# Moving small TensorE products into the beat of a recurrence step

## The chip, the cores and the metric

The kernel runs on one core of a Trainium2 chip. The metric is device time in microseconds (us) of one execution: 2334.18 us is the median of three runs of the kernel before, which lie between 2333.84 and 2334.26 us. The change does the same work; only the order in which its instructions are issued differs.

## The reference

Two layers work on 512 tokens of width 2048 in float32. The first layer projects the normalised input onto a forgetting attention (16 heads) and an RWKV-7 time mix (16 heads of size 64); the second is a gated MLP with a mixing over tokens. Each layer ends with an output projection, a second norm and a gated per-layer embedding. What the change touches is the time mix, which the reference writes as a scan over tokens with a 64x64 state `S` per head:

```python
def step(S, inp):
    r_t, w_t, k_t, v_t, kk_t, a_t = inp
    sa = jnp.einsum('bhij,bhj->bhi', S, kk_t)
    S = S * w_t[:, :, None, :] - sa[..., None] * (kk_t * a_t)[:, :, None, :] + v_t[..., None] * k_t[:, :, None, :]
    y = jnp.einsum('bhij,bhj->bhi', S, r_t)
    return S, y
```

Its outputs are normalised per head, a bonus term is added, and the result is gated and projected.

## The kernel before, in words

**Dense products.** Every projection is a stream of 128x128 weight blocks. SP loads a raw block, ACT rounds it to `whi` (L163), DVE computes the rest `wlo = raw - whi` (L165), and TensorE adds three products per block into a PSUM bank: `whi` with the high part of the activations (L179), `whi` with the low part (L180), `wlo` with the high part (L181). One such triple is called a **beat** here. One tile of `whi` or `wlo` holds four blocks, so it serves four beats, twelve dense matmuls; there are four buffers of each.

**The time mix by chunks.** The scan is turned into chunks of 64 tokens, two heads at a time, so a **period** is one of eight pairs of heads with eight chunks. For a pair there are:

- `rwkv_prep` (11 steps): decay, sigmoid gates, norms. Its products are the two LoRA products (L321) and a block sum (L302). On ACT it has a table load, sigmoids (L356, L360), a second table load (L332) and exponentials (L393, L398: `Pd`); on DVE among others the clamp of the block sum (L376), `kk` (L378), L382 and L383.
- `rwkv_ops` (4 steps for each half of the chunks): DVE alone, the scaled operands `BK` (L419, L420) and `AR` (L422, L425).
- `rwkv_head` (2 steps for each half): eight products of 64x128 tiles (L445) into two PSUM banks `tm` and `g`, and their masks on DVE (L449 to L462).
- `rwkv_inverse` (11 steps): inverts eight triangular 64x64 blocks for each head by doubling. A step is one burst of 32 products of 32x32 tiles (L512), four of them on different diagonal blocks behind each other; the result goes through DVE (`X` at L521, the transposed `T` at L529) and ACT (`R` at L530) into the next burst. The last two bursts have 16 products (L512 with `A` as an operand, and the last with `R` and `X`), and write `Tfin` through ACT (L541, L545; `X` by DVE at L538 and ACT at L539).
- `rwkv_tokens` (one step for each half): transposes to token-major form (L476, L484), copied by ACT (L478, L487, L488).
- `rwkv_chain` (three steps for each of eight chunks, 24 in a period): the recurrence. Step one is L558 and its copy `Bs` (DVE L561 and ACT L562), step two is L565 and its copy `UV` (L567, L568), step three is L573 with the new state `SV` (DVE L577), and the outputs L582 and L583.
- `rwkv_fin` (7 steps): head norm and bonus with block sums (L302).

**What sets the order.** The dense products carry a counter of beats. Each small step has a place, a number of beats, and `beat` runs every step whose place has come, right behind the dense triple of that beat:

```python
def beat(self):
    self.beats += 1
    while self.side and self.side[0][0] <= self.beats:
        self.side.pop(0)[1]()
```

The places are tables in units of `WIN` = 36 beats; a period is two of these, 72 beats. `CHAIN` puts a step of the chain every third beat. `STAGE` (inverse), `FIN`, `HEAD`, `TOKENS`, `PREP` and `OPS` hold the others; those with a 1 at the end are for the first period. All steps of all periods stand in one sorted list:

```python
def put(pr, n, step):
    todo.append((1 + 2 * WIN * pr + n, step))
```

So a period holds steps of four pairs at once: the chain of pair `pr`, the end (`FIN`) of pair `pr - 1`, heads and inverse of pair `pr + 1`, and the preparation of pair `pr + 2`. Behind this the Tile framework orders instructions by its own estimate of readiness and by priorities (copies of the chain and of the inverse are raised), so a step may be issued some matmuls away from its beat. The engines' queues then run in that order: an instruction that waits holds up those behind it.

Of the kernel before, what the change touches and what calls it, by code (L numbers as in the profile page):

```python
# [39 lines left out]

WIN = 36
even = lambda n, first, last: [WIN * (first + (last - first) * k / (n - 1)) for k in range(n)]
STAGE = even(11, 0.8, 1.94)
CHAIN = even(12, 0.06, 0.98), even(12, 1.06, 1.98)
FIN = even(7, 0.1, 0.9)
PREP = even(11, 1.3, 1.78)
PREP1 = even(11, 0.0, 0.24)
OPS = even(4, 1.83, 1.97), even(4, 0.06, 0.28)
OPS1 = even(4, 0.27, 0.38), even(4, 0.42, 0.56)
HEAD = even(2, 0.03, 0.18), even(2, 0.4, 0.6)  # L50
HEAD1 = even(2, 0.41, 0.48), even(2, 0.6, 0.7)
TOKENS = [1.03 * WIN], [0.02 * WIN]

WARM = 12

# [17 lines left out]
class Net:  # L73
# [542 lines left out]
    def rwkv_all(self, dense, first, wp, ps):  # L616
# [46 lines left out]
        def put(pr, n, step):  # L663
            todo.append((1 + 2 * WIN * pr + n, step))

        def run(pr, make, *args_places):
            *args, places = args_places
            gen = []

            def step():  # L670
                if not gen:
                    gen.append(make(*args))
                next(gen[0], None)

            for n in places:
                put(pr, n, step)
            put(pr, places[-1], lambda: [0 for _ in gen[0]])

        def begin(pr):
            S0 = sts[pr]["hf", 0]["SV"][:, 0]  # L680
            for q in range(2):
                nc.gpsimd.memset(S0[q * 64 : q * 64 + 64, q, :], 0.0)
            sts[pr]["Yt"] = self.t(wp, [P, T], "Yt")

        for pr in range(8):
            put(pr, CHAIN[0][0], lambda pr=pr: begin(pr))
            run(pr, tokens, pr, 1, TOKENS[1])
            for h in range(NG):
                run(pr, chain, pr, h, CHAIN[h])
            if pr > 0:  # L690
                run(pr, fin, pr - 1, FIN)
            if pr < 7:
# [4 lines left out]
                for h in range(NG):  # L697
                    run(pr, head, pr + 1, h, (HEAD if pr else HEAD1)[h])
                run(pr, inverse, pr + 1, STAGE)
                run(pr, tokens, pr + 1, 0, TOKENS[0])  # L700
            if pr < 6:
# [772 lines left out]
```

## Time and profile before

| what | us |
|---|---|
| median of three runs | 2334.18 |
| the profiled execution's own time | 2334.16 |
| its span, first to last instruction | 2332.5 |
| TensorE busy in the span | 2306.9 (99%) |
| VectorE (DVE) busy | 1234.6 (53%) |
| ScalarE (ACT) busy | 1043.2 (45%) |
| GpSimd (POOL) busy | 277.8 (12%) |
| first step of the chain, period 0 | starts at 142.2 |
| first step of the chain, periods 1 to 7 | 222.6, 296.7, 373.4, 447.4, 524.1, 598.2, 671.0 |
| last burst of the inverse (L512) | 666.2 |

The time outside the span is 1.7 us and is the same work in both kernels. The stretch that the tables shape runs from about 130 to 750 us. A matmul's end in the profile is modelled, so its start, and the distance to the next start, is what to read; "x64" behind L512 means 32 products, since every float32 product stands as two records.

### The profile page before, as it was taken

To read this page: it belongs to the slowest core of one execution; us is meant where nothing else is said; L and a number is where in the kernel's file an instruction comes from. 1 tells how busy PE (TensorE), PEld (TensorE's weight loads), DVE (VectorE), ACT (ScalarE), POOL (GpSimd) and SP (SyncE) were. 2 spreads that over 40 slices of the span, in tenths; PEclk is the share of its full clock that TensorE was granted. 3 is DMA by queue.
4 is the path that set the end of the run, shared out by engine and by line. 5 is a ranking of instruction groups with operands and counts; after the bars stand their busy time and mean duration, and the time that the engine had idled before them with its cause. 6 is when DMAs were issued, how large, how long until landed. Compare 5 with 4: busy or idle time off the path is not lost.

```text
span 2332.5 us, 38949 instructions
## 1 busy us (share of the span) xinstructions
PE 2306.9 (99%) x15380; PEld 1898.4 (81%) x15380; DVE 1234.6 (53%) x2526; ACT 1043.2 (45%) x2134; POOL 277.8 (12%) x314
## 2 busy tenths in 40 slices
PE   8999999999999999999999999999999999999999
PEld 7777887778887788778888888888888888888889
DVE  8665656656533877862246553237544443226433
ACT  5445554555443666753354343223333332335322
POOL 3111111111100000000112110003442000110000
PEclk9999999999999999999999999999999999999999
DMA  6322232223234533343333333334443332332332
GB/s 227 89 76 75 63 85 78 72 65 83 73 96 142 153 92 103 96 127 121 93 105 102 100 100 91 100 98 105 109 107 97 100 99 93 97 108 91 109 117 91
DMA packets 300341, 235.03 MB, mean 101 GB/s; under 512 B 11485, under 2 KB 251246, under 8 KB 299134
## 3 DMA queue, kind: packets, MB, share of 16 engines
q1 hardware_dynamic: 300158, 232.54, 34.3%
q8 instruction: 121, 1.98, 0.3%
q14 instruction: 62, 0.51, 0.1%
HBM read 216.47 MB, written 16.02 MB: 100 GB/s over the span
## 4 chain that ended last, share of the span: by engine, by line
PE 92%; DVE 4%; DMA 2%; ACT 2%; issue 1%; POOL 0%; SPq 0%; ACTq 0%; DVEq 0%; POOLq 0%
PE mm L179 16%; PE mm L181 15%; PE mm L180 15%; PE mm L940 6%; PE mm L939 6%; PE mm L941 6%; PE mm L218 5%; PE mm L217 5%; PE mm L216 5%; PE tm L512 2%; PE tm L855 1%; PE g L867 1%; DMA gz<-gd 1%; PE mm L1172 1%; DVE wlo L165 1%
## 5 line engine op out<-in xcount | busy, mean ns | idle before, releaser
L165 DVE TENSOR_TENSOR wlo<-raw,whi 128x512 fp32r<-128x512 f32 x720 | 516.5, 722 | 739.5 <-ACT whi L163 701.0
L163 ACT CAST whi<-raw 128x512 fp32r<-128x512 f32 x720 | 445.9, 621 | 889.4 <-PE mm L180 350.0
L179 PE MATMUL mm<-xh,whi 128*128 128x512 f32 x1120 | 468.3, 418 | 0.0
L181 PE MATMUL mm<-xh,wlo 128*128 128x512 f32 x1120 | 441.7, 394 | 1.2 <-DVE wlo L165 1.2
L180 PE MATMUL mm<-xl,whi 128*128 128x512 f32 x1120 | 439.2, 392 | 0.0
L181 PEld LDWEIGHTS mm<-xh,wlo 128*128 128x128 f32 x1120 | 210.2, 188 | 48.1 <-DVE wlo L165 1.6
L179 PEld LDWEIGHTS mm<-xh,whi 128*128 128x128 f32 x1120 | 211.5, 189 | 35.8
L180 PEld LDWEIGHTS mm<-xl,whi 128*128 128x128 f32 x1120 | 211.5, 189 | 31.9
L179 PE MATMUL mm<-yh,whi 128*128 128x512 f32 x576 | 225.9, 392 | 0.0
L181 PE MATMUL mm<-yh,wlo 128*128 128x512 f32 x576 | 224.4, 389 | 0.0
L180 PE MATMUL mm<-yl,whi 128*128 128x512 f32 x572 | 222.6, 389 | 0.0
L941 PE MATMUL mm<-xh,wlo 128*128 128x512 f32 x384 | 149.4, 389 | 0.0
L939 PE MATMUL mm<-xh,whi 128*128 128x512 f32 x384 | 149.4, 389 | 0.0
L940 PE MATMUL mm<-xl,whi 128*128 128x512 f32 x384 | 149.4, 389 | 0.0
L1094 POOL TENSOR_TENSOR accq<-accq,sq 128x512 f32<-128x512 f32 x42 | 56.7, 1349 | 608.7 <-ACT sq L1092 607.6
L181 PEld LDWEIGHTS mm<-yh,wlo 128*128 128x128 f32 x576 | 108.1, 188 | 22.8
L179 PEld LDWEIGHTS mm<-yh,whi 128*128 128x128 f32 x576 | 108.1, 188 | 22.1
L180 PEld LDWEIGHTS mm<-yl,whi 128*128 128x128 f32 x572 | 107.4, 188 | 22.0
L216 PE MATMUL mm<-whi,xh 128*128 128x512 f32 (+1 forms) x320 | 111.2, 347 | 0.0
L218 PE MATMUL mm<-whi,xl 128*128 128x512 f32 (+1 forms) x320 | 110.9, 347 | 0.0
L217 PE MATMUL mm<-wlo,xh 128*128 128x512 f32 (+1 forms) x320 | 110.9, 347 | 0.0
L216 PE MATMUL mm<-whi,yh 128*128 128x512 f32 x256 | 99.7, 389 | 0.0
(383 smaller groups left out, 3749.1 us busy)
## 6 DMA issues: line engine op xcount, KB each, us to landing
raw<-in_ab_w_in_dram SPq DMA_DIRECT2D x128, 512.0 KB, 4.0
raw<-in_c_w_in_dram SPq DMA_DIRECT2D x96, 512.0 KB, 3.7
raw<-in_ple_w_gate_dram SPq DMA_DIRECT2D x64, 512.0 KB, 3.9
raw<-in_ab_w_out_dram SPq DMA_DIRECT2D x32, 512.0 KB, 3.9
raw<-in_c_w_out_dram SPq DMA_DIRECT2D x32, 512.0 KB, 3.9
gd<-wlo SPq DMA_DIRECT2D x21, 256.0 KB, 2.2
xt<-in_x_dram SPq DMA_DIRECT2D x4, 1024.0 KB
xd<-xT SPq DMA_DIRECT2D x4, 1024.0 KB, 3.9
```

The lines of the kernel that those rows point to most:

```text
L163: nc.scalar.copy(hi[:, : m * n], src)
L165: self.weng.tensor_tensor(lo[:, : m * n], src, f(hi[:, : m * n]), ALU.subtract)
L179: nc.tensor.matmul(acc, hi, xhi[k], start=(k == 0), stop=False)
L180: nc.tensor.matmul(acc, hi, xlo[k], start=False, stop=False)
L181: nc.tensor.matmul(acc, lo, xhi[k], start=False, stop=(k == nk - 1))
L216: nc.tensor.matmul(accs[m][:, :n], xh, hi, start=(j == 0), stop=False)
L217: nc.tensor.matmul(accs[m][:, :n], xh, lo, start=False, stop=False)
L218: nc.tensor.matmul(accs[m][:, :n], xl, hi, start=False, stop=(j == nk - 1))
L939: nc.tensor.matmul(accs[j], hi[:, js], xhi[k], start=(k == 0), stop=False)
L940: nc.tensor.matmul(accs[j], hi[:, js], xlo[k], start=False, stop=False)
L941: nc.tensor.matmul(accs[j], lo[:, js], xhi[k], start=False, stop=(k == nk - 1))
L1094: eng.tensor_tensor(accq, accq, sq, ALU.add)
```

## The change

Four tables change, and a helper table appears. `BEHIND` is the list of the chain's 24 places, each plus 0.01 beat, so a step that is put there stands in the same beat as a step of the chain and behind it in the sorted list.

```diff
-STAGE = even(11, 0.8, 1.94)
 CHAIN = even(12, 0.06, 0.98), even(12, 1.06, 1.98)
-FIN = even(7, 0.1, 0.9)
+
+BEHIND = [n + 0.01 for half in CHAIN for n in half]
+STAGE = [0.6 * WIN, *BEHIND[8:18]]
+FIN = [4, BEHIND[2], 11, BEHIND[5], 20, 21, BEHIND[7]]
 PREP = even(11, 1.3, 1.78)
...
-HEAD = even(2, 0.03, 0.18), even(2, 0.4, 0.6)
+HEAD = [BEHIND[0], 6.5], [BEHIND[4], 20]
 HEAD1 = even(2, 0.41, 0.48), even(2, 0.6, 0.7)
-TOKENS = [1.03 * WIN], [0.02 * WIN]
+TOKENS = [BEHIND[20]], [BEHIND[1]]
```

In beats of a period: the eleven inverse steps stood at 28.8 to 69.84, every 4.1 beats, and stand at 21.6 and then 26.26 to 53.22, every third beat. The heads stood at 1.08 and 6.48, 14.4 and 21.6, and stand at 2.17 and 6.5, 14.21 and 20. The transposes of a pair's first half move from 37.08 to 62.26, those of the second half from 0.72 to 5.18. The seven end steps stood at 3.6, 8.4, 13.2, 18.0, 22.8, 27.6 and 32.4, and stand at 4, 8.19, 11, 17.22, 20, 21 and 23.25. `PREP` and `OPS` stay where they are. Instructions of each kind and their number are the same on every engine.

Counted over the order on PE from the first to the last step of the chain, the dense stream is broken by small products in 280 places before and in 223 after. Names below carry running numbers; line numbers of the change are two higher than those of the kernel before.

On PE, the end of the inverse in the third period: the 16 products of `T` with `A` (L512, L514 in the change), two matmuls behind a chain step before.

```order
L179 MATMUL mm_4553<-xh_80_298,whi_4556 128x512
L180 MATMUL mm_4553<-xl_81_299,whi_4556 128x512
L512 MATMUL tm_837_4579<-T_4532,A_684_3699 32x32 x15
L181 MATMUL mm_4553<-xh_80_298,wlo_4557 128x512
L179 MATMUL mm_4553<-xh_80_298,whi_4556 128x512
L180 MATMUL mm_4553<-xl_92_325,whi_4556 128x512
L181 MATMUL mm_4553<-xh_80_298,wlo_4557 128x512
L179 MATMUL mm_4553<-xh_80_298,whi_4556 128x512
L180 MATMUL mm_4553<-xl_94_339,whi_4556 128x512
L181 MATMUL mm_4553<-xh_80_298,wlo_4557 128x512
L558 MATMUL ch_4574<-SV_3685,AR_134_521 128x128
L512 MATMUL tm_837_4579<-T_4532,A_684_3699 32x32
```

```order
L183 MATMUL mm_4351<-xh_80_298,wlo_4355 128x512
L567 MATMUL ch_4417<-Bs_4363,Tfin_131_518 128x64
L514 MATMUL tm_796_4421<-T_4399,A_682_3693 32x32 x16
L181 MATMUL mm_4351<-xh_98_369,whi_4450 128x512
L182 MATMUL mm_4351<-xl_99_370,whi_4450 128x512
L323 MATMUL pp_4445<-LOp_175_705,lw_139_526 128x512
L323 MATMUL pp_4445<-LOp_175_705,lw_140_527 128x512
L183 MATMUL mm_4351<-xh_98_369,wlo_4451 128x512
```

The burst was cut into 15 products and one, seven matmuls apart; now its 16 stand together behind the chain's second step of chunk 5, 38 dense matmuls earlier in the period.

On ACT, the same period, from the chain's copy `Bs` of chunk 5 on (`sg` and `a` are sigmoids, `UV` and `Yt` copies of the chain, `lw` the LoRA weights, `Pd` the decay).

```order
L562 COPY Bs_4274<-ch_4272 64x64
L356 ACT_TABLE_LOAD
L356 ACTIVATE sg_4283<-pp_4280,col_125_501 128x512
L163 CAST whi_4556<-raw_4554 128x512
L313 CAST lw_139_526<-w2a_957_5258 128x128
L360 ACTIVATE a_4335<-pp_4332,col_125_501 128x512
L568 COPY UV_3684<-ch_4328 64x64
L332 ACT_TABLE_LOAD
L393 ACTIVATE sg_4548<-cum_4344 128x512
L398 ACTIVATE Pd_4566<-cum_4344 128x8x64
L584 COPY Yt_3727<-ch_4356 64x64
L585 COPY Yt_3727<-ch_4356 64x64
```

```order
L564 COPY Bs_4363<-ch_4361 64x64
L532 COPY R_4400<-tm_790_4366 128x256
L543 COPY Tfin_132_519<-R_4400 32x8x32
L358 ACT_TABLE_LOAD
L358 ACTIVATE sg_4409<-pp_4406,col_125_501 128x512
L165 CAST whi_4599<-raw_4597 128x512
L541 COPY X_4438<-tm_796_4421 32x256
L570 COPY UV_3748<-ch_4417 64x64
L543 COPY Tfin_132_519<-R_4400 32x8x32 x3
L362 ACTIVATE a_4448<-pp_4445,col_125_501 128x512
L334 ACT_TABLE_LOAD
L586 COPY Yt_3683<-ch_4469 64x64
```

The inverse's last copies (`R`, `Tfin`, `X`) now stand among the preparation's table loads and sigmoids, since `STAGE` ends where `PREP` runs. Behind the rows shown follow, in the change, L587 (`Yt`), L547 (`Tfin`), a `whi`, L547, L395, `Pd` (L400), two `lw` and the next `Bs`.

On DVE, the same period, from the clamp of the preparation's block sum on (`gn`), down to the new state `SV` of chunk 6.

```order
L376 TENSOR_SCALAR gn_4432<-pp_4429 128x512
L521 TENSOR_TENSOR X_4471<-tm_815_4438,idst_513 128x256
L378 TENSOR_TENSOR kk_4398<-kk_4398,gn_4432 128x512
L567 COPY UV_3684<-ch_4486 64x64
L382 TENSOR_SCALAR gn_4476<-a_4335,col_125_501,omka_575 128x512
L422 SCALAR_TENSOR_TENSOR AR_133_520<-kk_4398,Pd_4566 64x4x64
L383 TENSOR_TENSOR k_3655<-k_3655,gn_4476 128x512
L419 TENSOR_TENSOR BK_839_4603<-a_4335,sg_4548 64x4x64
L386 SCALAR_TENSOR_TENSOR rkb_4493<-r_3654,col_125_501,k_3655 128x512
L529 STREAM_TRANSPOSE T_4532<-tm_822_4499 128x256
L420 TENSOR_TENSOR BK_839_4603<-k_3655,sg_4548 64x4x64
L577 SCALAR_TENSOR_TENSOR SV_3685<-SV_3685,PC_2567,ch_4539 64x64
```

```order
L378 TENSOR_SCALAR gn_4527<-pp_4524 128x512
L569 COPY UV_3748<-ch_4546 64x64
L380 TENSOR_TENSOR kk_4493<-kk_4493,gn_4527 128x512
L384 TENSOR_SCALAR gn_4536<-a_4448,col_125_501,omka_575 128x512
L424 SCALAR_TENSOR_TENSOR AR_133_520<-kk_4493,Pd_4609 64x4x64
L385 TENSOR_TENSOR k_3655<-k_3655,gn_4536 128x512
L167 TENSOR_TENSOR wlo_4600<-raw_4597,whi_4599 128x512
L167 TENSOR_TENSOR wlo_4629<-raw_4597,whi_4628 128x512
L167 TENSOR_TENSOR wlo_4657<-raw_4654,whi_4656 128x512
L579 SCALAR_TENSOR_TENSOR SV_3749<-SV_3749,PC_2610,ch_4562 64x64 x2
L388 SCALAR_TENSOR_TENSOR rkb_4553<-r_3654,col_125_501,k_3655 128x512
```

The inverse's `X` and `T` are gone from this stretch, `rkb` and the operands `BK` stand later, and three `wlo` in a row stand between the preparation and `SV`; before, the three `wlo` followed the first `SV` row.

## Prediction

> **What bounds the kernel now.** I read the page's head first, then the busy time of the stretch that the tables shape, then what TensorE waited for in it, and last the order of time around single breaks.
>
> ```profile
> span 2332.5 us, 38949 instructions
> PE 2306.9 (99%) x15380; PEld 1898.4 (81%) x15380; DVE 1234.6 (53%) x2526; ACT 1043.2 (45%) x2134; POOL 277.8 (12%) x314
> ...
> PE 92%; DVE 4%; DMA 2%; ACT 2%; issue 1%; POOL 0%; SPq 0%; ACTq 0%; DVEq 0%; POOLq 0%
> ```
>
> TensorE sets the end, and there is little idle time on it to win. The change touches only the periods of the time mix; their busy time by stage:
>
> ```profile
> 130.00:670.00 540.00, 534.13 (x6554) 431.18 (x6553) 327.29 (x801) 283.40 (x695) 74.27 (x100) 1.00 0.27 75
> ```
>
> In these 540 us PE is busy for 534.1, at the full granted clock, so at most 5.9 us of waiting can go. The waits of PE in the same stretch say where it lies (total, times, longest):
>
> ```profile
> PE ch L565 <- ACT Bs L562: 1.5, 2, 0.7
> PE tm L512 <- DVE T L529: 1.2, 3, 0.4
> PE mm L181 <- DVE wlo L165: 1.2, 3, 0.4
> PE tm L445 <- DVE AR L422: 0.9, 1, 0.9
> PE tm L512 <- ACT X L539: 0.8, 1, 0.8
> ```
>
> The last two lie in the lead-in and in the first period, whose order on PE keeps those products apart as before. The first three are 3.9 us in steady periods: chain step two that waits for `Bs`, and the cut burst `T` with `A`, followed by a late `wlo`.
>
> Everything else that the change can alter is how PE's busy time is put together. So I priced a break in the dense stream from starts of matmuls (columns: start, modelled length, then the instruction). A dense matmul follows the one before it after 0.23 us.
>
> ```profile
> 347.82 0.40 PE L181 MATMUL mm<-xh,wlo 128*128 128x512 f32 x1
> 348.06 0.38 PE L573 MATMUL ch<-UV,BKt 128*128 128x128 f32 x2
> ...
> 348.82 0.75 PE L512 MATMUL tm<-R,X 32*32 32x32 f32 x64
> ...
> 349.84 0.40 PE L180 MATMUL mm<-xl,whi 128*128 128x512 f32 x1
> ...
> 356.74 0.40 PE L181 MATMUL mm<-xh,wlo 128*128 128x512 f32 x1
> 357.07 0.75 PE L512 MATMUL tm<-R,X 32*32 32x32 f32 x64
> 357.75 0.50 PE L179 MATMUL mm<-xh,whi 128*128 128x512 f32 x1
> 358.08 0.39 PE L180 MATMUL mm<-xl,whi 128*128 128x512 f32 x1
> ...
> 358.55 0.38 PE L573 MATMUL ch<-UV,BKt 128*128 128x128 f32 x2
> ...
> 359.45 0.40 PE L180 MATMUL mm<-xl,whi 128*128 128x512 f32 x1
> ```
>
> Here the same two groups stand once together and once apart. A burst of 32 products alone: 358.08 - 356.74 - 2 x 0.23 = 0.88 us. The chain's third step alone (L573, L582, L583): 359.45 - 358.08 - 3 x 0.23 = 0.68. Both in one break: 349.84 - 347.82 - 2 x 0.23 = 1.56. Together they cost what they cost apart, to the 0.02 us that these rows resolve. The first dense matmul behind a break takes 0.33 instead of 0.23 (357.75 to 358.08), but a small product that follows another pays the same in its place.
>
> **The change part by part.** No instruction is added or removed, on no engine; DMAs, SP's queue and table loads keep their number. Four terms remain.
>
> *Fewer breaks.* The order on PE has 223 breaks instead of 280, 57 less, at 0.02 us: -1.1 us. The bounds are 0 (the rows above as they stand) and 57 x 0.10 = 5.7 us (if each break paid its own restart of 0.33 - 0.23); I take the rows' resolution, since the measured pair shows next to nothing. [...]
>
> *Bursts that are cut or joined.*
>
> ```profile
> 360.28 0.69 PE L512 MATMUL tm<-T,A 32*32 32x32 f32 x30 [0.44 <-DVE T L529]
> 361.38 0.50 PE L181 MATMUL mm<-xh,wlo 128*128 128x512 f32 x1 [0.41 <-DVE wlo L165]
> ...
> 362.87 0.39 PE L181 MATMUL mm<-xh,wlo 128*128 128x512 f32 x1
> 363.10 0.38 PE L558 MATMUL ch<-SV,AR 128*128 128x128 f32 x2
> 363.41 0.24 PE L512 MATMUL tm<-T,A 32*32 32x32 f32 x2
> ...
> 363.92 0.39 PE L180 MATMUL mm<-xl,whi 128*128 128x512 f32 x1
> ```
>
> The one product cut off costs 363.92 - 362.87 - 2 x 0.23 - 0.23 (L558, a third of 0.68) = 0.36 us; it stands in three periods and joins its 15 fellows: -1.0 us. Against that the change cuts a head's eight products into one and seven in three periods. By busy time:
>
> ```profile
> 162.00:165.00 3.00, 1.16 (x8) 0.96 (x8) 1.00 0.00 0
> 308.00:311.00 3.00, 1.16 (x16) 0.97 (x16) 1.00 0.19 43
> ```
>
> Four products into one bank (x8 records) take 1.16 us, as long as eight into two banks in turn (x16): a pair runs side by side. A product without its partner so costs 0 to 1.16/4 = 0.29; near the upper end, 0.25 x 3 = +0.75 us.
>
> *Waits that go.* `Bs` for L565: the row that waited,
>
> ```profile
> 299.87 0.43 PE L565 MATMUL ch<-Bs,Tfin 128*128 128x64 f32 x2 [0.75 <-ACT Bs L562]
> ```
>
> came at the start of a period, where the masks of a head just before stood ahead of `Bs` on DVE. Now that head stands ten dense matmuls behind L558, and `Bs` ahead of its masks. `T` with `A` now has nine dense matmuls, a LoRA product and L565 behind the burst that makes `T` (2.1 + 0.5 + 0.2 = 2.8 us), and `T` stands right behind `Bs` on DVE. Both waits go, and the `wlo` that was late with them: -3.9 us. Bound: 0.
>
> *Waits that come.* What was late there was the preparation on DVE, and it still has to be done, now with the inverse's last copies in its queue on ACT. The rows:
>
> ```profile
> 343.38:349.58 6.20, 6.04 (x9) 1.00 0.37 102
> ...
> L541 ACT COPY Tfin<-R 32x256 f32<-32x256 f32 x8 | 3.2, 404 | 0.1
> L530 ACT COPY R<-tm 128x256 f32<-128x256 f32 x8 | 3.0, 370 | 2.4 <-DVE T L529 2.4
> L334 ACT ACTIVATE gn<-gn 128x512 f32<-128x512 f32 x2 | 1.3, 634 | 2.8 <-DVE gn L376 2.8
> L335 ACT ACTIVATE gn<-gn 128x512 f32<-128x512 f32 x2 | 1.3, 632 | 0.1
> L539 ACT COPY X<-tm 32x256 f32<-32x256 f32 x2 | 0.7, 365 | 1.1 <-DVE X L538 1.0
> ...
> 353.35 0.69 DVE L376 TENSOR_SCALAR gn<-pp 128x512 f32<-128x512 f32 x1 [1.02 <-PE pp L302]
> 355.40 0.69 DVE L378 TENSOR_TENSOR kk<-kk,gn 128x512 f32<-128x512 f32 x1 [0.91 <-ACT gn L335]
> 356.93 0.68 DVE L383 TENSOR_TENSOR k<-k,gn 128x512 f32<-128x512 f32 x1
> 360.65 1.88 DVE L165 TENSOR_TENSOR wlo<-raw,whi 128x512 fp32r<-128x512 f32 x3
> ```
>
> Take the order of the third period from chunk 5's L558 at 0. ACT reaches `R` when the burst (0.23 + 0.88) and `T` are through, and ends it at 2.0. From the first table load to `Pd` it needed 6.2 us for nine instructions; now one `lw` (0.2) goes out of that row and one `X` (0.4), six `Tfin` in all (6 x 0.4), two `Yt` (0.4) and a `whi` (0.6) come in: `Pd` at 2.0 + 6.2 - 0.2 + 0.4 + 2.4 + 0.4 + 0.6 = 11.8. DVE waits there: two `AR`, two `lw` and `PC` (1.5, an estimate from L422's kind of operation), L376 (0.7): 14.0. ACT L334 and L335: 15.3. DVE from L378 to L383 (355.40 to 357.61): 17.5. The first `wlo` (1.88/3): 18.1. PE needs it 47 dense matmuls behind that L558 (10.8), with ten chain products (2.3), a burst of 32 (0.9), two of 16 (1.5), three full-width pairs (1.4) and the transposes (0.7, taken as three chain products) on the way: 17.6. It is 0.5 late. Behind it stand two more `wlo` (1.25) and `SV` (0.5) while PE has seven dense matmuls (1.6): another 0.2. So 0.7 us in each of the three periods that have this order, +2.1; in the other three, two `wlo` stand ahead of the preparation, and I find 0.4 of slack. Those three begin with L573 only five dense matmuls behind L565 instead of nine; for that, between 0 and the 0.75 above, I take 0.15 each, +0.5. Bounds of the whole term: 0, and with 1.6 us more delay on ACT 10.5 + 0.5 (below).
>
> *Sum*, against the profiled execution's 2334.16 us (its span 2332.5 and 1.7 around it, untouched; the median 2334.18 is the same within 0.02): -1.1 - 1.0 + 0.75 - 3.9 + 2.1 + 0.5 = -2.65, so **2331.5 us**.
>
> **The rivals.** A measurement of this kernel tells about 0.2% from no change, 4.7 us: below 2329.5 is faster, above 2338.9 slower.
>
> A, *the restart is paid by the break*: 57 x 0.10 instead of 1.1 gives 2326.9. For it: 0.33 behind every break; against it: the pair that costs 1.56 both ways.
>
> B, *no new wait*: ACT's queue has idle time that I counted as work, or `wlo` runs further ahead; without the +2.6 it is 2328.9. For it: ACT is busy for only 283 of 540 us. Against it: the three `wlo` stand behind the preparation in one in-order queue, and this very tile was late before.
>
> C, *slower*: the preparation's chain ACT, DVE, ACT, DVE comes later than I added up. In the rows above ACT idled 2.4 us ahead of `R` and 2.8 ahead of L334 in two periods, each time for DVE; with 1.6 us of such waits inside the longer queue, `wlo` is 2.3 late in three periods and 1.6 - 0.4 = 1.2 in the other three: 10.5 in place of 2.1, 2339.9. Break-even with the gains is at a delay of about 0.6 us, slower by 0.2% at about 1.5.
>
> D, *the change hardly does what it says*: the framework still issues 223 breaks, LoRA products and block sums among them apart from any chain step, and the old waits reappear elsewhere at their old 3.9 us instead of 2.6 with the small terms used up; then 2334.
>
> **How the numbers follow.** The forecast, 2329.7 to 2333.5, has 0.50; D 0.13, A 0.10, B 0.14, C 0.13. Faster: A, B and 0.03 of the forecast's lower edge, 0.27. Slower: 0.11 of C. Within 0.2%: the rest, 0.62. The range takes in A's value and most of the way to C's: 2327 to 2338.
>
> **What would show it.** PE's rows for `T` with `A` and for L565 without a wait (right: -3.9); in the first, third and fifth period L181 waiting for `wlo` close behind L573, L476 and L484, then L558 for `SV` (right: 0.5 and 0.2; C: 2 us and more; B: none). A break with a burst behind a chain step still costs the sum of both (wrong: 0.10 less). Busy PE in the periods should fall by no more than 2 us. The forecast is wrong if the waits of PE there change by more than 4 us in total, or if busy time does.

## The result and the profile after

The changed kernel takes 2346.66 us (median; 2344.92 to 2350.48) against 2334.01 beside it, a ratio of 1.0056 [1.0046, 1.0066]: 12.7 us slower. The forecast was 2331.5, 2.7 us faster, with a range of 2327 to 2338, so both its sign and its range were wrong. The profiled execution of the change is its longest, 2350.48 us. Line numbers of the change, and of all kernels below, are two higher than those of the prediction.

The head of the profile's page, and the shares of the chain of work that ended last:

```profile
span 2348.8 us, 38961 instructions
PE 2313.1 (98%) x15380; PEld 1913.0 (81%) x15380; DVE 1239.4 (53%) x2526; ACT 1046.7 (45%) x2134; POOL 292.8 (12%) x314
...
PE 87%; DVE 6%; ACT 4%; DMA 2%; issue 1%; SPq 0%; POOL 0%; ACTq 0%; DVEq 0%; POOLq 0%
```

TensorE's part of the chain that ends last fell from 92% to 87%: waits for other engines now set more of the time. POOL's busy time rose from 277.8 to 292.8 us with the same work; no term of the prediction is about POOL.

The same 540 us as in the prediction, first the busy time of the engines, then PE's waits (total, times, longest):

```profile
130.00:670.00 540.00, 523.83 (x6479) 431.01 (x6478) 330.50 (x790) 278.14 (x676) 85.04 (x97) 0.99 0.27 73
```

```profile
PE ch L567 <- ACT Bs L564: 5.5, 7, 1.2
PE tm L486 <- DVE UV L569: 4.4, 2, 2.5
PE mm L183 <- DVE wlo L167: 1.6, 3, 0.5
PE tm L447 <- DVE BK L422: 1.6, 1, 1.6
PE tm L514 <- DVE X L523: 1.4, 3, 0.5
PE tm L486 <- ACT BKt L480: 0.7, 1, 0.7
```

PE stands idle for 16.2 us of the stretch instead of 5.9. The two largest rows are a chain step that waits for `Bs` (5.5 instead of 1.5 us, in other places than before) and L486, the transposes of `v` in `rwkv_tokens`, which waited nowhere before. The wait for `T` is gone. So the theory to test is that the two rows of `TOKENS`, the places of the transposes, cost the time.

**Theory T, the second transposes.** They moved from beat 0.72, ahead of the head (1.08), to 5.18, behind it (2.17). The order of time of all engines at the start of the third period:

```profile
303.38 0.61 PE L478 MATMUL tm<-ident,BKh 128*128 128x128 f32 x4
303.41 0.62 ACT L165 CAST whi<-raw 128x512 fp32r<-128x512 f32 x1 [4.29 <-PE mm L183]
304.06 0.69 DVE L167 TENSOR_TENSOR wlo<-raw,whi 128x512 fp32r<-128x512 f32 x1 [2.04 <-ACT whi L165]
...
305.10 0.43 DVE L461 TENSOR_TENSOR AR<-tm,strict 64x256 f32<-64x256 f32 x1
...
305.88 0.42 DVE L464 TENSOR_TENSOR GR<-tm,incl 128x256 f32<-128x256 f32 x1
...
306.45 0.41 PE L486 MATMUL tm<-ident,v 128*128 128x128 f32 x2 [2.46 <-DVE UV L569]
```

L486 writes the bank `tm` that the head's products filled. The last mask that reads the bank (`GR`, to 306.30) stands on DVE behind a `wlo`; that `wlo` waited 2.04 us for its `whi`, and the `whi` 4.29 us for PE's own L183. The row of L486 names `UV`, the copy next behind `GR` on DVE, but by the code L486 neither reads nor overwrites it. PE has 0.61 us of transposes between that L183 and L486, while the chain through ACT and DVE takes 3 (303.41 to 306.45).

**Theory P, POOL beside DVE.** The order of time some ten us earlier:

```profile
288.27 1.94 POOL L390 TENSOR_TENSOR a<-kk,a 128x512 f32<-128x512 f32 x1 [24.35 <-DVE gn L384]
...
289.58 1.18 DVE L388 SCALAR_TENSOR_TENSOR rkb<-r,col,k 128x512 f32<-128x512 f32 x1
...
290.18 1.49 POOL L473 TENSOR_TENSOR BKh<-BK,PC 128x512 f32<-128x512 f32 x1
...
290.69 1.25 DVE L421 TENSOR_TENSOR BK<-a,sg 64x256 f32<-64x256 f32 x1
...
294.17 0.22 DVE L563 COPY Bs<-ch 64x64 f32<-64x64 f32 x1
...
294.68 0.43 PE L567 MATMUL ch<-Bs,Tfin 128*128 128x64 f32 x2 [1.15 <-ACT Bs L564]
```

POOL's key scaling `BKh` (L473), the first instruction of `rwkv_tokens`, now follows `a` in POOL's queue and runs beside the operands `BK`. The `BK` that overlaps it takes 1.25 us, and `Bs`, four `BK` and one `AR` later on DVE, is late for PE by 1.15. Rival of both is theory S: the inverse's copies in the preparation's stretch (rival C of the prediction).

### The profile page after: what moved, and what is told of

Read it like the earlier page. It is cut to its first block, busy times and chain, and to the rows that moved or that the text cites. A ratio compares the mean times of both kernels' runs of the same rounds, so it can differ in the third digit from the quotient of the medians.

```text
span 2348.8 us, 38961 instructions
## 1 busy us (share of the span) xinstructions
PE 2313.1 (98%) x15380; PEld 1913.0 (81%) x15380; DVE 1239.4 (53%) x2526; ACT 1046.7 (45%) x2134; POOL 292.8 (12%) x314
## 4 chain that ended last, share of the span: by engine, by line
PE 87%; DVE 6%; ACT 4%; DMA 2%; issue 1%; SPq 0%; POOL 0%; ACTq 0%; DVEq 0%; POOLq 0%
PE mm L181 15%; PE mm L182 14%; PE mm L183 14%; PE mm L941 6%; PE mm L943 6%; PE mm L942 6%; PE mm L218 5%; PE mm L220 5%; PE mm L219 5%; PE tm L514 2%; DVE wlo L167 1%; PE tm L857 1%; PE g L869 1%; DMA raw<-in_ab_w_in_dram 1%; ACT whi L165 1%
## 5 line engine op out<-in xcount | busy, mean ns | idle before, releaser
L183 PE MATMUL mm<-xh,wlo 128*128 128x512 f32 x1120 | 442.7, 395 | 1.7 <-DVE wlo L167 1.6
L183 PEld LDWEIGHTS mm<-xh,wlo 128*128 128x128 f32 x1120 | 210.9, 188 | 50.5 <-DVE wlo L167 3.4
L183 PE MATMUL mm<-yh,wlo 128*128 128x512 f32 x576 | 224.4, 389 | 0.0
L183 PEld LDWEIGHTS mm<-yh,wlo 128*128 128x128 f32 x576 | 108.1, 188 | 23.0
```

Of the source, the lines that this page charges most:

```text
L183: nc.tensor.matmul(acc, lo, xhi[k], start=False, stop=(k == nk - 1))
```

## The experiments

Each kernel was timed beside the kernel before (2333.44 to 2333.87 us). "Over before" is the difference of the medians of a kernel and of the kernel before beside it; the change stands at +12.65, and a **gain** below is what a run takes off that.

**One table or row undone at a time.**

```diff
 second_old
-TOKENS = [BEHIND[20]], [BEHIND[1]]
+TOKENS = [BEHIND[20]], [0.02 * WIN]
 first_old
-TOKENS = [BEHIND[20]], [BEHIND[1]]
+TOKENS = [1.03 * WIN], [BEHIND[1]]
 stage_old
-STAGE = [0.6 * WIN, *BEHIND[8:18]]
+STAGE = even(11, 0.8, 1.94)
 head_old
-HEAD = [BEHIND[0], 6.5], [BEHIND[4], 20]
+HEAD = even(2, 0.03, 0.18), even(2, 0.4, 0.6)
```

> The change with the transposes of a pair's second half put back from beat 5.18 to 0.72, ahead of the head. Theory T (the transposes now wait for the bank tm, which the head's products behind which they stand have just filled and whose masks stand on DVE behind wlo tiles): the waits of L486 for UV and BKt, 5.1 us in the change, go, and with them the two stretches of half clock right behind them (some 1.7 us each): 8 us faster than the change, 2338 to 2339. Theory S (the inverse's copies among the preparation's, as rival C of the prediction has it): the transposes' place matters little, 2345 to 2347.

> The change with the transposes of a pair's first half put back from beat 62.26 to 37.08. Theory P (their key scaling on POOL now runs beside the preparation's tail and the operands BK and AR on DVE, which come late, with the chain's copy Bs behind them): the waits of L567 for Bs in the changed periods, 5.5 us in the change, fall to 2 or less, 3 to 4 us faster than the change, 2343. Theory T alone: the waits of L486 stay, and the time with them, 2345 to 2347; theory S: the same 2345 to 2347.

> The change with the inverse's steps put back to every 4.1 beats, 28.8 to 69.84. Theory S: the preparation is no longer late, and most of the loss goes with it: 2336 to 2339. Theory T: the waits of L486 stay, and the inverse's own waits and cut burst of the kernel before come back: 2346 to 2349.

> The change with the head's steps put back to beats 1.08, 6.48, 14.4 and 21.6. Theory T: a head's first step still stands ahead of the second transposes (1.08 against 5.18), but its masks have 1.1 beats more: the waits of L486 shrink from 5.1 us to 3 or 4, 2343 to 2346. If the head's place behind the first chain step is itself the cause (its masks ahead of Bs on DVE), the waits of L567 for Bs go too and it is 2338 to 2341. Theory S: no change, 2346 to 2347.

Measured, in this order: 2338.44 us (ratio to before 1.0020 [1.0011, 1.0029], +4.6 us), 2340.46 (1.0032 [1.0023, 1.0041], +6.6), 2343.97 (1.0040 [1.0028, 1.0053], +10.1), 2342.65 (1.0036 [1.0023, 1.0048], +8.8). PE's waits with the second transposes back:

```profile
PE ch L567 <- ACT Bs L564: 5.0, 7, 1.1
...
PE tm L447 <- DVE AR L424: 0.9, 1, 0.9
```

and with the first transposes back:

```profile
PE tm L486 <- DVE UV L569: 4.0, 2, 2.1
PE mm L183 <- DVE wlo L167: 3.8, 6, 0.8
```

Each row of `TOKENS` removes its own wait and leaves the other: without the late second transposes no L486 waits, without the late first ones no wait for `Bs` is left in this stretch. The gains are 8.1 and 6.1 us; the first is as T forecast, the second larger than P's 3 to 4. Not all of the 8.1 is the wait for the bank: in the lead-in, at 156 us, the head's products (L447) wait 1.6 us in the change and 0.9 with the second transposes back, and the 3.4 us at half clock behind that wait (last section) go too.

Putting the inverse back gives only 2.6 us where S asked for 8 or more, and more than T allowed. Its trace shows why it is no clean test of S: the old inverse still runs at beat 62, where the first transposes now stand, and they wait for its bank.

```profile
PE tm L486 <- ACT R L532: 5.2, 6, 0.9
```

In the same trace the waits for `Bs` are down to 1.0 us. So `Bs` is late only with both the new transposes and the new inverse in place; undoing either removes most of that wait.

With the head 1.1 beats earlier the waits of L486 go altogether, more than expected, and 3.9 us with them; those for `Bs` stay (5.6), and so does the lead-in's 1.6 with its 3.4 us at half clock. That is the nearest to a price of L486's wait alone: about half of the 8.1.

**The transposes' table as the only change, and as the only thing undone.**

```diff
 tok_old: the change with
+TOKENS = [1.03 * WIN], [0.02 * WIN]
 only_tok: the kernel before with
+TOKENS = [BEHIND[20]], [BEHIND[1]]
 tokhead_old: as tok_old, and
+HEAD = even(2, 0.03, 0.18), even(2, 0.4, 0.6)
```

> The change with both transposes put back to 37.08 and 0.72. Theories T and P together: the 8.2 and 6.2 us that the two gave one at a time add up to 14.4 and the rest of the change is worth what the prediction's small terms say: 2331 to 2333.5. Theory S (inverse and preparation in one stretch cost something too): a loss stays, 2336 to 2339.

> The kernel before with the transposes' table alone changed. If the transposes carry the loss by themselves: PE's waits up by 8 us or more, 2341 to 2346. If it takes the inverse in the preparation's stretch as well: 2335 to 2338.

> The change with both transposes and the four head steps put back, so that only the inverse and the end steps are new. If the head's place right behind a chain step costs something by itself (its masks stand on DVE ahead of what the chain needs): 1 to 3 us faster than with the transposes alone put back. If not: within 1 us of it. Theory S as there: 2336 to 2339.

Without the moved transposes the change takes 2334.12 us, 1.0002 [0.9993, 1.0011]: no different from before, 0.6 us later than the forecast's upper end. The moved transposes alone, in the kernel before, cost 8.0 us, a time as expected (2341.45, 1.0030 [1.0018, 1.0042]). Their waits are others than in the change: 5.2 us of L486 behind the old inverse as in `stage_old`, and only 1.0 for `Bs`; PE's idle time in the 540 us rose by 3.7 us, not by 8, and 6.8 us at half clock (157 to 165 us) are in this execution as well. So the loss belongs to `TOKENS`, 12.0 of 12.65 us in the change; by which waits, depends on what stands beside it. What the rest of the change leaves of waits:

```profile
PE mm L183 <- DVE wlo L167: 3.8, 6, 0.8
PE tm L514 <- DVE X L523: 1.0, 2, 0.5
```

With the heads put back too it is slower again, 2337.89 us (1.0017 [1.0008, 1.0026]), where I expected it faster or level. Two waits for `Bs` (1.6 us) are back in its trace at the start of a period, so the head's new place is what had removed them; the profiled execution, 2336.34, doesn't show the rest of the 3.8 us, which stays open.

**T by itself: another bank, another place.**

```diff
 own_bank
-        pv = self.t(ps, [P, GC // 2, P], self.tm())
+        pv = self.t(ps, [P, GC // 2, P], "pp" if h else self.tm())
 second_late
-TOKENS = [BEHIND[20]], [BEHIND[1]]
+TOKENS = [BEHIND[20]], [BEHIND[3]]
```

> The change with every table as it is, but the second transposes of a pair's second half (L486) write the bank pp, which stands empty there, in place of a tm bank. Theory T (what costs is the wait for the bank that the head's masks still read): the waits of L486, 5.1 us, go without any step moved, and with them the half clock behind the longest: 2338 to 2340, as with the transposes put back. Rival (the transposes' and copies' place at beat 5.18 itself, or the stretch before it): less than 2 us better than the change, 2345 to 2347.

> The change with the second half's transposes at beat 11.2, behind the first chain step of chunk 1's successor and clear of the head's masks (head's second step at 6.5), instead of 5.18. Theory T (the wait is for the masks of the head between whose products and masks the transposes now stand): the waits of L486 in the even periods go, 2338 to 2340.5, as with the place ahead of the head. Rival (behind a chain step the transposes and their five copies on ACT cost that wherever they stand): waits of 3 us or more move to beat 11, 2344 to 2347.

The other bank gave nothing, 2346.15 us (1.0057 [1.0043, 1.0071]). L486 waits no longer, so the bank is what held it; but the block sum of `rwkv_fin` (L304) uses `pp` too and stands behind the transposes, and it now waits for their copies:

```profile
PE pp L304 <- ACT SV L490: 4.1, 7, 0.7
```

The wait was passed on, and the run can't say what L486 alone costs. At beat 11.2, clear of the masks, L486 doesn't wait either, but the gain is only 2.7 us (2343.39, 1.0039 [1.0027, 1.0052]) instead of the 6 or more that T forecast. In the lead-in the head's two products now wait 1.4 and 1.2 us where the change waits 1.6, PE's clock is at half behind them for about 6.8 us instead of 3.4, and 1.5 us of waits for `UV` (L575) are new.

```profile
PE tm L447 <- DVE BK L422: 1.4, 1, 1.4
PE g L447 <- DVE AR L424: 1.2, 1, 1.2
```

**P by itself: another buffer, no key scaling, and the control.**

```diff
 bkh3
-    "r": 2, ... "BKt": 2, ...
+    "r": 2, ... "BKt": 2, "BKh": 3, ...
 no_bkh, before_no_bkh (in the kernel before), second_no_bkh (with second_old's table)
-        BKh = self.t(wp, [P, GC, P], "BKh")
-        nc.gpsimd.tensor_tensor(
-            BKh, BK.rearrange("p c a t -> p c (a t)"), PC.broadcast_to([P, GC, P]), ALU.mult
-        )
+        if not hasattr(self, "zk"):
+            self.zk = self.t(wp, [P, GC, P], "BKh", bufs=1)
+            nc.gpsimd.memset(self.zk, 0.0)
+        BKh = self.zk
```

> The change with a third buffer for the scaled keys BKh (L473): the second half's BKh then stands on POOL ahead of the preparation's product a (L390) and no longer runs, 1.49 us, right behind it beside the operands BK on DVE. Theory P (POOL's work beside DVE's makes BK late and so the chain's copy Bs): the waits of L567 for Bs, 5.5 us in the change, fall to 2.5 to 4, and the kernel is 1.5 to 3 us faster than the change, 2343.5 to 2345. Rival (the transposes on PE and their copies on ACT at beat 62 are the cause): the waits stay within 0.5 us, 2346 to 2347.

> The change without the key scaling: POOL's 16 products BKh (L473) are left out, the transposes read a tile of zeros instead (the chunks then pass no state on); every queue but POOL's is as in the change. Theory P (POOL's products run beside DVE's and slow them: BK 1.25 us beside BKh and 0.41 without): BK stands 0.8 to 1.2 us earlier, the waits of L567 for Bs in the changed periods fall from 5.5 to 1.5 or less, and the masks behind which L486 waits come earlier too, since a wlo stands beside BKh there; 4 to 6 us faster than the change, 2340.5 to 2343. Rival (Bs stands behind six operations of BK and AR, and their number and not their length is what costs): the waits stay above 4, 2345 to 2347.

> Control: the kernel before, without the key scaling on POOL (as in the run of the change without it; the chunks pass no state on). If the 7.2 us that leaving BKh out gave in the change come from BKh's new place beside the preparation: 0 to 2 us faster than before here (BKh beside AR, 1.38 us, is all there is), 2331.5 to 2333.5. If BKh costs as much wherever it runs: 2326 to 2328.

> The change with the second transposes put back to 0.72 and no key scaling on POOL. Theories T and P as two causes that do not touch each other: 8.2 and 7.2 us off the change, 2331 to 2333, with the waits of L486 and those of L567 in the changed periods both gone. If they overlap (both are DVE being late): 2334.5 to 2338.

A third buffer gained nothing (2346.79 us, 1.0053 [1.0040, 1.0065]), where P forecast 1.5 to 3 us, though the waits for `Bs` fell to 3.9 us: the transposes wait longer instead (6.2 us, was 5.1), and in the place where `Bs` waits longest `BKh` only slid on to the next `BK`, which it slows nearly as much.

```profile
292.63 1.09 POOL L473 TENSOR_TENSOR BKh<-BK,PC 128x512 f32<-128x512 f32 x1 [1.20 <-DVE BK L422]
292.84 1.17 DVE L421 TENSOR_TENSOR BK<-a,sg 64x256 f32<-64x256 f32 x1
```

Without the key scaling the change takes 2339.47 us (1.0024 [1.0016, 1.0033]), a gain of 6.6 us. The shortest, median and longest `BK` (ns) from 200 to 670 us, in the change and then without the scaling, show what went:

```profile
L421 DVE TENSOR_TENSOR BK<-a,sg x24: 406/423/1254, 218.1 to 605.0; 64x256 f32<-64x256 f32 x24
```

```profile
L421 DVE TENSOR_TENSOR BK<-a,sg x24: 406/422/609, 214.9 to 596.0; 64x256 f32<-64x256 f32 x24
```

and PE's waits without it

```profile
PE tm L486 <- DVE UV L569: 4.0, 2, 2.4
PE ch L567 <- ACT Bs L564: 1.6, 4, 0.6
...
PE tm L486 <- DVE GR L464: 0.8, 1, 0.8
```

The waits for `Bs` fall from 5.5 to 1.6, close to what P forecast. L486 still waits 4.0 + 0.8 us, so POOL is not what holds it; I had expected that in part. The control says how much of the 6.6 is the new place: the kernel before gains 2.2 us by the same omission (2331.35, 0.9992 [0.9983, 1.0000]). So `BKh`'s new place costs 6.6 - 2.2 = 4.4 us. With the 8.1 of the second transposes that is 12.5 of the 12.65. The sum is closer than its parts allow: by the intervals each part is known to about 3 us, `TOKENS` as a whole is 12.0, and the first transposes alone gave 6.1. Both at once bring the kernel back to before's time, 2333.09 us (0.9999 [0.9990, 1.0008]), without a wait of L486 and with 1.1 us for `Bs`; that is 13.1 of the 14.7 us that the two gave one at a time, so they overlap little.

**Two attempts at a better kernel.**

```diff
 best1
+STAGE = [0.6 * WIN, *BEHIND[7:17]]
+TOKENS = [1.03 * WIN], [BEHIND[3]]
 before_act (the kernel before), tok_old_act (with both transposes back)
-        nc.gpsimd.tensor_tensor(
-            BKh, BK.rearrange("p c a t -> p c (a t)"), PC.broadcast_to([P, GC, P]), ALU.mult
-        )
+        for e in range(GC):
+            nc.scalar.activation(BKh[:, e], BK[:, e].rearrange("p a t -> p (a t)"), AF.Copy, scale=PC[:, e, 0:1])
```

> First transposes back at 37.08, second at 11.2, and the inverse three beats earlier (23.25 to 50.2), so that its last copies on ACT end ahead of most of the preparation. If the waits for wlo (3.8 us with both transposes put back) come from those copies in ACT's queue: they fall to 1.5 or less, 2330 to 2332.5. If they come from the preparation's own chain: 2333.5 to 2335.

> Both transposes put back, and the key scaling done by ACT in four pieces (L474) in place of POOL, so that no BKh runs beside DVE. If POOL's work beside DVE costs something in the old places too and ACT has room: 1 to 2.5 us faster than with the transposes alone put back, 2331.5 to 2333. If ACT's queue has no room ahead of Bs and whi: 2335 to 2339.

> The kernel before with the key scaling done by ACT in four pieces in place of POOL. As there: 2331.5 to 2333 if ACT has room, 2335 to 2339 if not.

The inverse three beats earlier halves the waits for `wlo` (3.8 to 1.9 us), so about half of them come from its place; that it is its copies on ACT is likely but not shown, since its work on DVE moved as well. With the second transposes at 11.2 the lead-in's waits of 1.4 and 1.2 us are back, and the kernel takes 2336.95 us (1.0013 [1.0004, 1.0023]), outside both forecasts. The scaling on ACT leaves the change without its transposes where it was (2333.43, 1.0000 [0.9991, 1.0009]). In the kernel before it is worth 2.3 us, as much as leaving the scaling out: 2331.19, 0.9990 [0.9981, 0.9999], the only kernel here with all its work that is faster than before, by little. Of PE's waits from 130 to 670 us, the row for `Bs` fell from 1.5 to

```profile
PE ch L567 <- ACT Bs L564: 0.3, 1, 0.3
```

## Why the prediction was wrong, step by step

**The step that failed** is the sentence "Four terms remain": the moved transposes got no term of their own, that is 0, without a reason, and measured 12.0 us. They entered the sum only as time on PE ("0.7, taken as three chain products"), though the move also takes `BKh` and two copies past others in POOL's queue, five copies past others in ACT's, and a write to a bank past the head's masks. Neither the bank's readers nor POOL's queue stands in any term or rival. What the two cost is worked out above: 8.1 us for the place of the second transposes, part of it the wait for the bank, and 4.4 for the new place of `BKh`. How the 8.1 divides stays open. The trace of before had shown the effect of POOL's queue in small, two `AR` in 1.80 us instead of 2 x 0.42 beside `BKh` (line numbers of before):

```profile
294.01 1.38 POOL L471 TENSOR_TENSOR BKh<-BK,PC 128x512 f32<-128x512 f32 x1 [10.63 <-PE tm L476]
294.41 1.80 DVE L425 TENSOR_TENSOR AR<-r,Pd 64x256 f32<-64x256 f32 x2
```

**Fewer breaks, -1.1, and rival A.** A burst and the chain's third step in one break of the change:

```profile
348.04 0.39 PE L183 MATMUL mm<-xh,wlo 128*128 128x512 f32 x1
348.27 0.38 PE L575 MATMUL ch<-UV,BKt 128*128 128x128 f32 x2
...
349.03 0.75 PE L514 MATMUL tm<-T,AM 32*32 32x32 f32 x64
...
350.05 0.39 PE L182 MATMUL mm<-xl,whi 128*128 128x512 f32 x1
```

350.05 - 348.04 - 2 x 0.23 = 1.55, against 1.56 for the sum of both apart: so joining two groups saves next to nothing, as predicted, and A, which asks for 0.10 less, is refuted by this pair. Whether 57 of them are worth 1.1 us or nothing these rows can't tell.

**Joined and cut bursts, -1.0 and +0.75.** Not measured apart. Everything but the transposes together is +0.6 us by tok_old, with an interval of -1.6 to +2.6; the sum of the prediction, -2.65, lies outside. So the rest of the sum was too hopeful as well, by some 3 us.

**Waits that go, -3.9.** Right: without the transposes no wait for `T` is left, none for `Bs` at a period's start, and in the change itself "both waits go" holds for the places that were named. That `Bs` would be late elsewhere was the error. The lead-in, which the prediction took to stay as it was, didn't: its head waits 1.6 us instead of 0.9, and with the second transposes back 0.9 again.

**Waits that come, +2.6.** The ledger of ACT and DVE was right in kind: `wlo` is late in the first, third and fifth period by 0.5 in the change, as added up. It was short in size: by the trace without the moved transposes these waits are 3.8 us in all, 0.8 each in the periods named and, in place of "0.4 of slack", 0.5 each in the other three; and 1.0 for `X` came on top. The fall-back of 0.2 for `SV` shows once.

**The rivals.** C had the sign and 2339.9 us but another mechanism: the preparation behind ACT's longer queue. In tok_old its waits for `wlo` are 3.8 us and not 10.5, and the rest of the change makes up for them. B (no new wait) is refuted by them. D is refuted for the change by 16.2 us of idle time instead of 5.9; without the moved transposes its outcome, the old waits replaced by others (7.6 us idle, 2334.12 us), is what was measured, though not for its reason. No rival held a move whose cost lies on POOL or in a bank.

## What to carry to other kernels

When a step is moved, list every instruction it issues on every engine and every bank it writes, and look up for each who stands ahead of it in the new place: the cheapest-looking step here, two places of transposes, cost nearly all the time. A product that reuses a bank must stand far enough behind the products that filled it for their readers, with all that queues ahead of these readers, above all where one of those waits for TensorE itself: L486 waited up to 2.46 us here, with a `whi` in that queue that had waited 4.29 for L183. Work on POOL is not free because POOL is idle: `BK` took 1.25 us beside it instead of 0.42, so place it where DVE's critical operations are not.

## What the runs showed of the hardware

**POOL and DVE.** Two operations of DVE that read two tiles in SBUF each, in the trace of before (count, then shortest, median and longest in ns):

```profile
L386 DVE SCALAR_TENSOR_TENSOR rkb<-r,col,k x6: 735/736/739, 208.4 to 585.3; 128x512 f32<-128x512 f32 x6
L419 DVE TENSOR_TENSOR BK<-a,sg x24: 416/420/423, 208.1 to 589.0; 64x256 f32<-64x256 f32 x24
```

In the change `rkb` takes 1.18 us beside POOL's `a`, and `BK` 1.25 beside `BKh`, while `X`, which reads a PSUM bank, doesn't vary, beside POOL's masks `AM` (0.74 us from 256.37, `X` from 256.26) or not (269.82):

```profile
L523 DVE TENSOR_TENSOR X<-tm,idst x24: 416/425/426, 251.8 to 657.3; 128x256 f32<-128x256 f32 x24
```

In the rows of theory P `BK` starts at 290.69 and ends at 291.94, 0.27 us after `BKh`. How POOL's work holds up DVE's, no run shows. What a slow operation costs depends on what waits for it: in first_old `rkb` takes 1.18 us as well (from 287.94), and no wait for `Bs` is left in the 540 us.

**The clock.** Around some of PE's long waits the granted clock fell to 0.50 for some 3.4 us. A dense matmul then follows the one before it after 0.43 us (307.99 to 309.69 for four) instead of 0.23, so I estimate 3.4 x (1 - 0.23 / 0.43), some 1.6 us, as lost each time. The change around the wait of 2.46 us (columns: stretch, its length, busy PE, PEld, DVE, ACT, POOL, clock, DMA share, GB/s):

```profile
305.00:307.00 2.00, 0.55 (x4) 0.54 (x5) 1.91 (x8) 1.15 (x4) 0.66 (x1) 1.00 0.00 0
307.00:309.00 2.00, 2.00 (x8) 1.59 (x7) 1.18 (x3) 1.56 (x5) 0.39 (x1) 0.67 0.00 0
309.00:311.00 2.00, 2.00 (x10) 1.81 (x9) 0.56 (x2) 0.00 (x0) 0.40 (x1) 0.50 0.48 109
311.00:313.00 2.00, 2.00 (x10) 1.65 (x10) 0.00 (x0) 1.63 (x5) 0.00 (x0) 0.98 0.51 154
```

It is not certain: the wait of 1.93 us at 462 us of the same execution has none behind it, and the one of 1.6 us at 156 has. Without the key scaling, a wait of 2.43 us at 302 has none either. Three such stretches (157, 307 and 792 us) are by this estimate about 5 us of the 16.3 by which this execution's span is longer than that of before, and a fourth at 21 us is 0.5 (the products from 19.61 to 24.39, in before from 19.42 to 23.72); the 10.3 us more of waits are most of the rest. The stretch at 792 begins within a wait of 1.6 us (to 792.89) that the kernel before has too (to 777.53), there without half clock. The median execution is 3.8 us shorter than this one; its trace isn't kept, so its share stays open.

What decides which wait the half clock comes with, no run shows.
